# Seven-product FFN input on one Trainium2 core: Silu as one ScalarE function, a bank sum done by TensorE, no arithmetic on POOL, casts issued ahead of functions

## The chip, the cores and the metric

The kernel runs on one core of a Trainium2 chip. Its engines are called as in the profile: PE (matmul) with its weight loads PEld, DVE (VectorE), ACT (ScalarE), POOL (GpSimd) and SP, which only issues transfers. The metric is the device time of one execution in microseconds (us); of several runs the median counts.

## The reference, cut to what matters

One decoder layer over 512 tokens and 1024 channels, in float32: a hybrid mixer, then a SwiGLU FFN with 2816 hidden channels. The change is in the FFN's first half, in the end of the mixer that feeds it, and in one line for a row of the FFN's second half.

```
x = x + gate1 * rms_norm(mix_out, g_post_mix)
h2 = rms_norm(x, g_pre_ffn) * (1 + scale2) + shift2
gt, up = split(h2 @ w_ffn_in, 2)          # 1024 -> 2 x 2816
f = (silu(gt) * up) @ w_ffn_out
x = x + gate2 * rms_norm(f, g_post_ffn)
```

## The kernel before, in words

Every float32 product is made of three float32r matmuls (`mm3`, L156): each operand is taken apart into a rounded high part, cast by ACT, and the rest, a subtraction on DVE (`split`, L152 to 154: the cast is L153, the subtraction L154). So each piece of weights costs a cast of 128x1024 and a subtraction of 128x1024 before PE can use it. High and low parts live in tiles `whi` and `wlo`, four buffers each.

**The stage of the change.** `h2 @ w_ffn_in` is done in 11 units `u` of 2 x 128 hidden channels (gate and up columns together). A unit is a 2x2 by 2x2 block product (two halves of the 1024 inputs, two halves of the tokens, two column blocks), and it is done in seven block products instead of eight. A product is one call `step(u, q, ...)`, q = 1 to 7: 24 matmuls of 128x256 at L1185 into one bank of PSUM. The order of the 77 products is written out by hand in `WINO` (L243). Counted from 0, steps 0 to 13 belong to units 0 and 1 and the first two products of unit 2, step 14 is (u=0, q=3), and from step 27 on seven steps per unit run in one fixed order.

- The weights of a unit come by DMA from SP's queue (`wino_load`, L257) into four blocks. Products 1, 2, 4 use a block as it is. Products 5, 6 and 3 use a running sum `wsum` of blocks: first the sum of two (L281), then two more, each added by an accumulating DMA that POOL issues (L302). Product 7 uses a block to which another was added (`wsum3`, L285).
- `step` first prepares a later piece (`split_to`, cast and subtraction), then runs `flush()` for what was put off, then its 24 matmuls.
- The token side: `hbh`/`hbl` hold four blocks of token parts; `tx` holds the parts of three combinations that are built from `ta` (the tile `tar`) and `b22` (tile `b`) while the first products run.
- The results: `gated` (L1189) makes silu(g)*u as Exp, Ln(1+.), Exp on ACT (`sigm`, L163 to 165: g's sigmoid), then two DVE products put off to the next step (L1194, L1195). `gated_m1` (L1206) combines three banks on DVE (c, L1209 to 1212) ahead of it. In the loop over units from 3 on, product 1 is copied to the SBUF tile `u` by ACT (L1367), and product 6 is taken from it by DVE (L1374).

**Ahead of the stage** the last two of four token blocks leave the mixer's output projection: `chain_sq`, `chain_norm`, `chain_x1` (L1091 the residual, L1095 its product with the scale row, named `xm`), `chain_norm2`, `chain_h2` (L1104) and four transposes per half (`h2_tr`). For block 2 both `xm` products run on POOL, for block 3 one of them. In the first units the sums L281 and L285 and the combinations L1312 and L1327 run on POOL too; from unit 2 on L281 and L285 run on DVE.

**Behind the stage** the FFN's second half, `f @ w_ffn_out`, runs over two halves of the output columns. During the first one a generator `mods_in_turn` (L972) makes the row of gate2 in two pieces; a `pump()` after each pair of weight blocks (24 matmuls of 128x512) lets it go on to its next `yield`. It adds up `macc` on DVE (L1002), has a bias added by an accumulating DMA from POOL (L1008), splits the result (`mah`) and multiplies it with ones on PE (L979, tile `pmr`). At the very end, for each of four token blocks, ACT makes Square sums, Ln (L1442) and Exp (L1444), DVE two products (L1447), and the result goes out.

The order on PE, DVE, ACT and POOL is that of the program in this stage (`manual_schedule`); each engine runs its instructions in that order. Where an instruction waits, all behind it on its engine waits as well.

## Time and profile before

| what | value |
|---|---|
| median of 3 runs | 853.81 us (849.71 to 855.4) |
| the profiled execution | 852.54 us, span 850.8 us |
| mean granted PE clock | 0.972 |
| PE busy | 771.2 us, 91% |
| DVE busy | 570.2 us, 67% |
| ACT busy | 423.1 us, 50% |
| POOL busy | 165.7 us, 19% |

The span is the time from the first to the last instruction; the execution lies 1.7 us around it. Busy time of PE counts overlapping, pipelined matmuls, so a busy PE isn't a PE at its peak; the number of matmuls that a stretch holds tells more. PEclk is the share of its clock that PE was granted. In rows of instructions the order is start and duration (us), engine, line, operation, output <- input, and in brackets how long the engine had been idle and who released it. In rows that group instructions the order is line, engine, operation, names and shapes, count, then busy us and mean ns of one, then idle time before them and who ended it.

### The profile page before, as it was taken

How to read it: one execution, taken by the hardware profiler on the slowest of the kernel's cores; microseconds unless marked ns; L12 is line 12 of the kernel's file. 1: busy time of each engine (PE TensorE's matmuls, PEld its weight loads, DVE VectorE, ACT ScalarE, POOL GpSimd, SP SyncE). 2: the span in 40 equal slices, each digit the busy share in tenths (PEclk: the TensorE clock that was granted, in tenths of full speed). 3: DMA queues.
4: the chain of work that ended last, by engine and by line, in shares of the span. 5: the costliest groups of instructions: out<-in, count | busy, mean ns of one | idle time of the engine just before them, and what ended most of it. 6: DMA issues, size and time to landing. Idle time of an engine off the chain costs nothing. (4 is left out here: it accounts for less than half of the span.)

```text
span 850.8 us, 11361 instructions
## 1 busy us (share of the span) xinstructions
PE 771.2 (91%) x4357; PEld 659.6 (78%) x4357; DVE 570.2 (67%) x808; ACT 423.1 (50%) x710; POOL 165.7 (19%) x200
## 2 busy tenths in 40 slices
PE   3899999999999999999975759999898889879996
PEld 3679887776788888888875659989888888768885
DVE  5989867568566664557878766767766767673214
ACT  5466544666674554516743534644455456333112
POOL 4353423244311111030035201111110110000000
PEclk9999999999999999999988869999999999999999
DMA  9962332214146877567652464666555444652202
GB/s 281 302 213 75 123 99 59 86 55 148 50 131 228 217 242 210 178 155 260 201 133 49 75 149 99 149 149 148 134 122 123 95 99 161 219 184 80 75 1 99
DMA packets 119462, 120.37 MB, mean 141 GB/s; under 512 B 4012, under 2 KB 93152, under 8 KB 119408
## 3 DMA queue, kind: packets, MB, share of 16 engines
q1 hardware_dynamic: 109072, 99.63, 38.2%
q0 software_dynamic: 9568, 18.96, 12.0%
q10 hardware_dynamic: 768, 1.07, 0.3%
q8 instruction: 34, 0.56, 0.3%
q14 instruction: 20, 0.16, 0.1%
HBM read 102.33 MB, written 2.10 MB: 123 GB/s over the span
## 5 line engine op out<-in xcount | busy, mean ns | idle before, releaser
L154 DVE TENSOR_TENSOR wlo<-wraw,whi 128x1024 fp32r<-128x1024 f32 (+1 forms) x129 | 160.6, 1251 | 125.0 <-ACT whi L153 124.9
L153 ACT CAST whi<-wraw 128x1024 fp32r<-128x1024 f32 (+1 forms) x129 | 132.3, 1031 | 132.7 <-PE pgt L158 33.2
L1185 PE MATMUL pf<-hbh,whi 128*128 128x256 f32 x352 | 101.9, 290 | 19.4 <-ACT hbh L153 9.7
L1185 PE MATMUL pf<-tx,whi 128*128 128x256 f32 x528 | 99.7, 290 | 12.7 <-ACT whi L153 9.0
L1185 PE MATMUL pf<-hbh,wlo 128*128 128x256 f32 x352 | 100.7, 286 | 4.5 <-DVE wlo L154 4.5
L1185 PE MATMUL pf<-hbl,whi 128*128 128x256 f32 x352 | 100.4, 285 | 1.8 <-DVE hbl L154 1.7
L1185 PEld LDWEIGHTS pf<-tx,whi 128*128 128x128 f32 x528 | 84.4, 196 | 13.6 <-ACT whi L153 9.4
L1185 PEld LDWEIGHTS pf<-hbh,whi 128*128 128x128 f32 x352 | 68.0, 193 | 22.5 <-ACT hbh L153 9.9
L1185 PE MATMUL pf<-tx,wlo 128*128 128x256 f32 x264 | 77.8, 295 | 7.0 <-DVE wlo L154 7.0
L157 PE MATMUL pgt<-hh,whi 128*128 128x512 f32 x192 | 75.8, 395 | 0.0
L159 PE MATMUL pgt<-hh,wlo 128*128 128x512 f32 x192 | 75.4, 393 | 0.0
L158 PE MATMUL pgt<-hl,whi 128*128 128x512 f32 x192 | 74.8, 389 | 0.0
L1185 PEld LDWEIGHTS pf<-hbh,wlo 128*128 128x128 f32 x352 | 67.8, 193 | 5.8 <-DVE wlo L154 5.8
L1185 PEld LDWEIGHTS pf<-hbl,whi 128*128 128x128 f32 x352 | 68.0, 193 | 2.4 <-DVE hbl L154 2.3
L302 POOL DMA_DIRECT2D wsum<-wraw x22 | 26.4, 1200 | 220.2 <-DVE wlo L154 211.0
L157 PE MATMUL pfo<-whi,fparts 128*128 128x512 f32 x154 | 61.2, 398 | 0.0
L158 PE MATMUL pfo<-wlo,fparts 128*128 128x512 f32 x154 | 61.2, 398 | 0.0
L159 PE MATMUL pfo<-whi,fparts 128*128 128x512 f32 x154 | 61.0, 396 | 0.0
L1185 PEld LDWEIGHTS pf<-tx,wlo 128*128 128x128 f32 x264 | 51.5, 195 | 10.5 <-DVE wlo L154 10.5
L154 DVE TENSOR_TENSOR wlo<-wsum,whi 128x1024 fp32r<-128x1024 f32 x33 | 40.2, 1222 | 17.0 <-ACT whi L153 17.0
L1002 DVE SCALAR_TENSOR_TENSOR macc<-wraw,sc,macc 128x512 f32<-128x512 f32 x56 | 42.8, 765 | 10.0 <-ACT macc L1000 5.5
L153 ACT CAST whi<-wsum 128x1024 fp32r<-128x1024 f32 x33 | 33.7, 1045 | 29.6 <-DVE wsum L281 21.1
(400 smaller groups left out, 1723.3 us busy)
## 6 DMA issues: line engine op xcount, KB each, us to landing
wraw<-in_w_in_dram SPq DMA_DIRECT2D x20, 1024.0 KB, 5.2
wraw<-in_w_ffn_in_dram SPq DMA_DIRECT2D x40, 512.0 KB, 5.9
wraw<-in_mod_w_dram SPq DMA_DIRECT2D x16, 1024.0 KB, 5.9
wsum<-wraw POOLq DMA_DIRECT2D x22, 512.0 KB, 5.9
...
wraw<-in_mod_w_dram SPq DMA_DIRECT2D x16, 512.0 KB, 6.5
...
gate<-gate POOLq DMA_DIRECT2D x14, 256.0 KB, 4.2
```

What stands on the lines that cost most here:

```text
L153: act.copy(hi, src)
L154: vec.tensor_tensor(lo, src, hi.bitcast(F32), ALU.subtract)
L157: pe.matmul(o, whi, xhi, start=start, stop=False)
L158: pe.matmul(o, whi, xlo, start=False, stop=False)
L159: pe.matmul(o, wlo, xhi, start=False, stop=stop)
L302: nc.gpsimd.dma_start(un["s"], un[0][q - 5], accum_op=ALU.add)
L1002: vec.scalar_tensor_tensor(acc, mw[:, r], c_, acc, op0=ALU.mult, op1=ALU.add)
L1185: pe.matmul(o[:, cs], a_[:, g, k, :], b_, start=(start and g + k + part == 0), stop=(stop and k == 3 and part == 2), skip_group_check=True)
```

## The change

It has seven parts.

1. **Silu.** `gated` calls one ACT function, Silu, and one DVE product; before it was three functions and two products. The function itself is put off to the next `flush`, its product to the one after. A table of functions with Silu is loaded once in the stage.
2. **The bank sum.** From unit 3 on ACT copies bank p1 to a fresh bank p6, product 6 accumulates onto it, and ACT copies the sum to SBUF. The DVE subtraction is gone; the sign goes into the token combination `ta`. Products 2 and 7 trade places.
3. **No arithmetic on POOL.** The `xm` products and the combinations of `ta` go to DVE. For units 0 and 1 the sums L281 and L285 become DMAs: SP loads one block straight into the `wsum` tile, POOL issues accumulating DMAs for the rest.
4. **Casts ahead of functions.** `split(..., True)` issues only the cast and puts the subtraction off to the next `lows()`; `begin(n)` prepares the pieces up to number n at the place where it stands. So in the first units casts stand on ACT ahead of functions and copies that came before them.
5. **Order.** The first six products are taken as (0,1), (1,1), (0,2), (2,1), (1,2), (2,2), and some of units 2 and 3 trade places. The sums of unit 2 and later are made one piece ahead.
6. The generator for the gate2 row waits one more `yield` between the DMA of its bias and its split.
7. With another table of functions loaded in between, the build places table loads before each Ln and each Exp at the end of the kernel.

Where the lines of the changed kernel differ from those before, L1225 is the Silu, L1226 its product, L155 the cast, L157 and L159 the subtraction, L1427 and L1434 the copies of the bank, L301, L302 and L315 the accumulating DMAs, L1488 the Square sums, L1503 and L1505 Ln and Exp.

POOL's queue over the whole stage, before:

```order
L1095 TENSOR_TENSOR xm<-x_3361,SHSC 128x512 x3
L281 TENSOR_TENSOR wsum<-wraw 128x1024
L302 DMA wsum<-wraw 128x2x512
L281 TENSOR_TENSOR wsum<-rawf 128x1024
L302 DMA wsum<-wraw 128x2x512
L285 TENSOR_TENSOR wraw<-wraw 128x2x512
L1312 TENSOR_TENSOR tar<-tar,b_3803 128x512 x2
L285 TENSOR_TENSOR rawf<-rawf,wraw 128x1024
L302 DMA wsum<-wraw 128x2x512
L1327 TENSOR_TENSOR tar<-braw,tar 128x512 x2
L302 DMA wsum<-wraw 128x2x512 x19
```

and of the change:

```order
L301 DMA wsum<-wraw 128x2x512
L302 DMA wraw<-wraw 128x2x512
L301 DMA wsum<-rawf 128x1024
L302 DMA rawf<-wraw 128x2x512
L315 DMA wsum<-wraw 128x2x512 x22
```

The eleven operations on tiles are gone, and 26 accumulating DMAs stand where 22 stood.

ACT in the loop over units, around unit 6 (three functions each for one block of 512 and two of 256 columns, with the casts of pieces between), before:

```order
L163 ACTIVATE sg_5722<-c_5718 128x512
L164 ACTIVATE sg_5722<-sg_5722,one_c 128x512
L165 ACTIVATE sg_5722<-sg_5722 128x512
L153 CAST whi<-wraw 128x1024
L163 ACTIVATE sg_5756<-pf_5588 128x256
L164 ACTIVATE sg_5756<-sg_5756,one_c 128x256
L165 ACTIVATE sg_5756<-sg_5756 128x256
L153 CAST whi<-wraw 128x1024
L153 CAST whi<-wsum 128x1024
L163 ACTIVATE sg_5823<-u_5589 128x256
L164 ACTIVATE sg_5823<-sg_5823,one_c 128x256
L165 ACTIVATE sg_5823<-sg_5823 128x256
```

and of the change, one whole unit (end of unit 4 to unit 5):

```order
L1225 ACTIVATE sg_4974<-pf_4839 128x256
L155 CAST whi<-wraw 128x1024
L1225 ACTIVATE sg_5011<-c_5000 128x512
L155 CAST whi<-wsum 128x1024
L155 CAST whi<-wraw 128x1024
L1225 ACTIVATE sg_5074<-u_4939 128x256
L1427 COPY pf_5100<-pf_5069 128x512
L155 CAST whi<-wraw 128x1024
L155 CAST whi<-wsum 128x1024
L1434 COPY u_5169<-pf_5100 128x512
L155 CAST whi<-wsum 128x1024
L155 CAST whi<-wraw 128x1024
```

Nine functions became three, one copy became two, and no three functions in a row stand between two casts any more.

ACT at the end of the kernel, for the last token block, before:

```order
L1427 ACTIVATE tt,so<-pfo3a 128x256
L1427 ACTIVATE tt,so<-pfo3b 128x256
L1442 ACTIVATE so<-so 128x1
L1444 ACTIVATE so<-so 128x1
L1452 DMA out_dram<-x_3361 128x512
```

and of the change:

```order
L1488 ACTIVATE tt,so<-pfo3a 128x256
L1488 ACTIVATE tt,so<-pfo3b 128x256
L1503 ACT_TABLE_LOAD
L1503 ACTIVATE so<-so 128x1
L1505 ACT_TABLE_LOAD
L1505 ACTIVATE so<-so 128x1
L1513 DMA out_dram<-x_3361 128x512
```

Two table loads per token block are new, eight in all.

The diff, cut to its core:

```diff
-    def split(hi, lo, src):
+    lows_ = []
+
+    def split(hi, lo, src, defer=False):
         act.copy(hi, src)
-        vec.tensor_tensor(lo, src, hi.bitcast(F32), ALU.subtract)
+        if defer:
+            lows_.append(lambda: vec.tensor_tensor(lo, src, hi.bitcast(F32), ALU.subtract))
+        else:
+            vec.tensor_tensor(lo, src, hi.bitcast(F32), ALU.subtract)
+
+    def lows():
+
+        while lows_:
+            lows_.pop(0)()
...
-    WINO = [(u, q) for u in range(3) for q in (1, 2)]
+    WINO = [(0, 1), (1, 1), (0, 2), (2, 1), (1, 2), (2, 2)]
     WINO += [(u, q) for q in (5, 7, 6, 4) for u in range(2)]
-    WINO += [(0, 3), (2, 5), (1, 3), (2, 4), (2, 7), (2, 6)]
-    WINO += [(3, 5), (3, 1), (3, 4), (2, 3), (3, 6), (3, 7), (3, 2)]
+    WINO += [(0, 3), (2, 5), (1, 3), (2, 4), (3, 5), (2, 6), (3, 1), (2, 7), (3, 4), (2, 3)]
+    WINO += [(3, q) for q in (6, 2, 7)]
     for u in range(4, NU):
-        WINO += [(u, 5), (u - 1, 3)] + [(u, q) for q in (1, 4, 6, 7, 2)]
+        WINO += [(u, 5), (u - 1, 3)] + [(u, q) for q in (1, 4, 6, 2, 7)]
...
+    def wsum_tile():
+        return late_pool["fx"].tile([P, 2, 512], F32, tag="wsum", name="wsum", bufs=2)
+
+    def wsum(u):
+
         un = units[u]
-        un["s"] = late_pool["fx"].tile([P, 2, 512], F32, tag="wsum", name="wsum", bufs=2)
-        eng.tensor_tensor(un["s"], un[1][0], un[1][1], ALU.add)
-
-    def wsum3(u, eng):
+        un["s"] = wsum_tile()
+        if u > 1:
+            vec.tensor_tensor(un["s"], un[1][0], un[1][1], ALU.add)
+            return
+        for g in range(2):
+            nc.sync.dma_start(un["s"][:, g].rearrange("p (k n) -> p k n", k=4),
+                              wino_src(u, 1, g)[:, 0:4])
+        nc.gpsimd.dma_start(un["s"], un[1][1], accum_op=ALU.add)
+        nc.gpsimd.dma_start(un[1][0], un[0][0], accum_op=ALU.add)
+
+    def wino_piece(u, q, defer=False):
         un = units[u]
-        eng.tensor_tensor(un[1][0], un[1][0], un[0][0], ALU.add)
-
-    def wino_piece(u, q):
-        un = units[u]
-        for i in range(2 if u > 2 else q in (1, 2)):
+        for i in (1, 0) if u > 2 and q != 3 else range(q in (1, 2)):
             if i not in un:
                 wino_load(u, i)
-        if q == 5 and u > 1:
-            wsum(u, vec)
-        if u > 1 and q == (7 if u == 2 else 4):
-            wsum3(u, vec)
         src = {1: (0, 0), 2: (0, 1), 4: (1, 1), 7: (1, 0)}.get(q)
         src = un[src[0]][src[1]] if src else un["s"]
         hi = wp.tile([P, 1024], FR, tag="whi", name="whi").rearrange("p (g n) -> p g n", g=2)
         lo = wp.tile([P, 1024], FR, tag="wlo", name="wlo").rearrange("p (g n) -> p g n", g=2)
-        split(hi, lo, src)
+        split(hi, lo, src, True)
         if q in (5, 6):
-            nc.gpsimd.dma_start(un["s"], un[0][q - 5], accum_op=ALU.add)
+            lows_.append(lambda: nc.gpsimd.dma_start(un["s"], un[0][q - 5], accum_op=ALU.add))
+        if not defer:
+            lows()
+
+        i = WINO.index((u, q)) + 1
+        nxt = WINO[i] if i < len(WINO) else (0, 0)
+        if nxt[1] == 5 and nxt[0] > 1:
+            for k in (1, 0) if nxt[0] > 2 else ():
+                if k not in units[nxt[0]]:
+                    wino_load(nxt[0], k)
+            wsum(nxt[0])
+        if u > 1 and q == 6:
+            vec.tensor_tensor(un[1][0], un[1][0], un[0][0], ALU.add)
...
             nc.gpsimd.dma_start(acc[0:1, :], mod_b[n0:n0 + 512].unsqueeze(0), accum_op=ALU.add)
             yield
+            if not rest:
+                yield
             am = parts_()
             split(*am, acc)
...
-    def chain_x1(tb, pos, junk, engs=(vec, vec)):
-        st, xms[tb] = sts[tb], []
-        xvs = [x1[:, tb, half(hf)] for hf in range(2)]
-        for hf, xv in enumerate(xvs):
+    def chain_x1(tb, pos, junk):
+        st = sts[tb]
+        for hf in range(2):
+            xv = x1[:, tb, half(hf)]
             vec.scalar_tensor_tensor(xv, pos[hf], st[:, 2:3], xv, op0=ALU.mult, op1=ALU.add)
             act.activation(junk(), xv, AF.Square, accum_out=st[:, 3 + hf:4 + hf])
-        for hf, xv in enumerate(xvs):
-            xms[tb].append(q2("xm"))
-            engs[hf].tensor_tensor(xms[tb][hf], xv, SC[hf], ALU.mult)
+
+    def chain_xm(tb):
+        xms[tb] = [q2("xm") for _ in range(2)]
+        for hf in range(2):
+            vec.tensor_tensor(xms[tb][hf], x1[:, tb, half(hf)], SC[hf], ALU.mult)
...
+        go, later[:] = later[:], []
+        for f_ in go:
+            f_()
...
-        sigm(sg, g)
-
-        def products():
-            vec.tensor_tensor(dst, sg, g, ALU.mult)
-            vec.tensor_tensor(dst, dst, u, ALU.mult)
-        later.append(products)
+        def function():
+            s_ = sg()
+            act.activation(s_, g, AF.Silu)
+            later.append(lambda: vec.tensor_tensor(dst, s_, u, ALU.mult))
+        later.append(function)
...
+        def begin(n):
+
+            while at["split"] < wino0 + n:
+                split_piece(True)
...
+        act.preload_act_table_set("silu_and_others")
+        fresh(5)
         tx_tiles(7)
         for u in range(2):
             vec.tensor_tensor(k4(t3_, u), k4(b22, u), pts[u][0], ALU.subtract)
-            parts_of(7, t3_, u)
-        for u in range(2):
-            pool.tensor_tensor(k4(ta, u), k4(ta, u), k4(b22, u), ALU.add)
-        f4s.append(f4_tile("f4"))
-        gated_m0(f4s[0], pb_[1][0], 0)
-        fresh(5, 3)
-        wsum3(1, pool)
-        for u in range(1, 3):
+            parts_of(7, t3_, u, True)
+        lows()
+        begin(9)
+        for u in range(3):
             f4s.append(f4_tile("f4"))
             gated_m0(f4s[u], pb_[1][u], 0)
             flush()
-        fresh(5, 3)
...
+            vec.scalar_tensor_tensor(k4(ta, u), k4(ta, u), -1.0, k4(b22, u), op0=ALU.mult,
+                                     op1=ALU.subtract)
...
+            vec.tensor_tensor(k4(ta, u), raws2[1, u], k4(ta, u), ALU.add)
...
+            p6 = bank("pf6")
+            act.copy(p6, p1)
             p4 = bank("pf4")
             step(u, 4, p4, True, True)
             if u == 3:
-                third()
-            p6 = bank("pf6")
-            step(u, 6, p6, True, True)
-            vec.tensor_tensor(u2, u2, p6, ALU.subtract)
+                third_of(2, pb_[5][2], u2s[2])
+            step(u, 6, p6, False, True)
+            u2 = temp("u2", 512, 2)
+            act.copy(u2, p6)
+            step(u, 2, p1, False, True)
+            gated_m0(f4s[u], p1, 0)
             p7 = bank("pf7")
             step(u, 7, p7, True, True)
             gated_m1(f4s[u], p4, p5, p7, u2)
-            step(u, 2, p1, False, True)
-            gated_m0(f4s[u], p1, 0)
-            third = lambda args=(u, p5, u2): third_at(*args)
+            third = lambda a_=(u, p5, u2): third_of(*a_)
```

139 lines of the change are left out of this document (80 added, 59 removed).

## The prediction

> **What bounds the kernel now.** I read the share of each engine first (PE busy 91% of the span), then cut the span into stages and read the busy time of every engine in each.
>
> ```profile
> core 0: us, PE busy (x) PEld busy (x) DVE busy (x) ACT busy (x) POOL busy (x), PEclk, DMA share, GB/s
> 425.87:510.84 84.97, 54.83 (x375) 52.48 (x373) 60.19 (x68) 36.65 (x68) 24.96 (x16) 0.80 0.45 100
> 519.34:547.60 28.26, 28.26 (x242) 28.26 (x241) 21.48 (x27) 13.71 (x19) 3.60 (x3) 1.00 0.76 159
> 547.60:711.30 163.70, 148.31 (x1182) 141.50 (x1181) 115.28 (x140) 84.54 (x123) 15.61 (x13) 1.00 0.56 131
> 570.90:594.20 23.30, 21.14 (x170) 20.15 (x169) 16.48 (x20) 11.69 (x18) 2.40 (x2) 1.00 0.60 136
> 711.30:850.80 139.50, 126.51 (x600) 103.50 (x598) 64.30 (x81) 42.98 (x70) 2.79 (x4) 0.98 0.32 110
> ```
>
> The second row holds steps 18 to 27 of the FFN input, ten times 24 matmuls, without a gap: 28.26/10 = 2.826 us is what a step costs when PE never waits. All 77 steps and two times eight transposes (1.04 us each, below) would take 220 us. They take 285 (425.87 to 711.30), so 65 us of this stage aren't PE's own work, in two parts. Steps 0 to 14, the first row, take 85 us instead of 44. Steps 28 to 76, the third, take 163.7 instead of 49 x 2.826 = 138.5, though DVE (115 of 163.7) and ACT (85) are far from full: there PE waits for the latency of a chain, not for an engine's rate. What it waits for, in the first part and then in the second:
>
> ```profile
> PE pf L1185 <- ACT hbh L153: 9.7, 1, 9.7
> PE pf L1185 <- ACT whi L153: 8.8, 1, 8.8
> PE pf L1185 <- ACT u L1268: 5.2, 2, 4.5
> ...
> PE pf L1185 <- DVE wlo L154: 10.7, 20, 0.9
> PE pf L1185 <- ACT whi L153: 3.7, 7, 0.6
> ```
>
> In the first part the waits have a price beyond themselves: after one, PE runs at half its clock.
>
> ```profile
> 469.29 0.80 PE L1185 MATMUL pf<-tx,whi 128*128 128x256 f32 x2 [8.81 <-ACT whi L153]
> 506.16 0.58 PE L1185 MATMUL pf<-hbh,whi 128*128 128x256 f32 x1 [9.65 <-ACT hbh L153]
> 505.00:510.00 5.00, 3.70 (x15) 3.41 (x16) 3.21 (x4) 2.05 (x3) 0.00 (x0) 0.50 0.01 3
> ```
>
> Step 14 goes on at 506.16 and step 15 starts at 510.84, the end of the first row: 4.7 us for most of a step. What made the 8.8 us is seen on DVE and POOL:
>
> ```profile
> 457.46 8.22 DVE L154 TENSOR_TENSOR tx<-t3r,tx 128x256 fp32r<-128x256 f32 x2 [0.47 <-ACT tx L153]
> 466.75 0.43 DVE L154 TENSOR_TENSOR tx<-t3r,tx 128x256 fp32r<-128x256 f32 x1 [0.47 <-ACT tx L153]
> L1312 POOL TENSOR_TENSOR tar<-tar,b 128x512 f32<-128x512 f32 x2 | 2.9, 1701 | 0.0
> L285 POOL TENSOR_TENSOR wraw<-wraw 128x1024 f32<-128x1024 f32 x1 | 2.9, 2857 | 0.0
> L285 POOL TENSOR_TENSOR rawf<-rawf,wraw 128x1024 f32<-128x1024 f32 x1 | 2.8, 2762 | 0.0
> ```
>
> Two subtractions that take 0.43 us each take 8.22 us while POOL runs those three groups (8.6 us) without a break. DVE stands still behind POOL, ACT waits for DVE, PE for both.
>
> **The change part by part: steps 0 to 14.** Without POOL's arithmetic DVE has more to do and no stall. Its durations in this stretch, and three rows that the count needs:
>
> ```profile
> 410.11 1.04 PE L1112 MATMUL pt<-ident,xm 128*128 128x128 f32 x8
> ...
> 424.52 1.22 DVE L154 TENSOR_TENSOR wlo<-wraw,whi 128x1024 fp32r<-128x1024 f32 x1
> ...
> 428.12 0.20 ACT L1077 ACTIVATION_READ_ACCUMULATOR sq<-pwo 128x1 f32 x1
> ...
> L154 DVE TENSOR_TENSOR wlo<-wsum,whi 128x1024 fp32r<-128x1024 f32 x8 | 9.7, 1223 | 4.3 <-ACT whi L153 4.3
> L154 DVE TENSOR_TENSOR tx<-tar,tx 128x256 fp32r<-128x256 f32 x8 | 2.9, 419 | 0.0
> L1104 DVE SCALAR_TENSOR_TENSOR xm<-xm,st,SHSC 128x512 f32<-128x512 f32 x4 | 2.8, 747 | 2.4 <-ACT st L150 2.4
> L1212 DVE TENSOR_TENSOR c<-pf,c 128x512 f32<-128x512 f32 x2 | 1.4, 692 | 0.2
> L1194 DVE TENSOR_TENSOR f<-sg,pf 128x256 f32<-128x256 f32 x3 | 1.3, 419 | 2.1 <-ACT sg L165 2.1
> ```
>
> Step 14 needs the second half of `hbl` from `b22`, which stands on DVE behind both chains c of units 0 and 1. From 425.7, where the subtraction for step 1 ends (424.52 + 1.22), I count what stands on DVE up to there: 14 subtractions of 128x1024 (14 x 1.22 = 17.1); one sum `wsum` (1.2); of 128x512 four xm, two products with G, eight token combinations (`tar`, `t3r`), four hbl, two u, six c, one f, 27 in all (27 x 0.69 = 18.6); seven with a scalar operand, four h2 and three x1 (7 x 0.75 = 5.2); twelve subtractions for tx (12 x 0.42 = 5.0); three f of 256 (1.3); three tiny ones (0.5). The sum is 48.9 us, so step 14 can't go on before 474.6. PE's own steps end earlier (13 x 2.826 + 2 x 1.04 from 428.7, the end of step 0, is 467.5): DVE is the bound here.
>
> The other end: DVE was idle for 84.97 - 60.19 = 24.8 us of this stretch; if all of that stays, step 14 goes on at 499.4. I walked the written order and put 6 us of waits on DVE, near the early end: 0.5 for the cast of product (0,2), 1.1 for the cast after `wsum` of unit 2, 1 for the table load of Silu, 3 for the second bank of sums. That last one is new: SP may load the `wsum` tiles once DVE's first product with G for block 3 has run, about 429.3 now (the squares ahead of it end at 428.3); twelve issues follow, and then POOL's accumulating DMAs, the third of which makes the sum for product (1,5).
>
> ```profile
> rawf<-in_w_ffn_in_dram SPq DMA_DIRECT2D x8, 256.0 KB, 5.0
> wsum<-wraw POOLq DMA_DIRECT2D x2, 512.0 KB, 5.1
> ```
>
> Its inputs are issued by 434.5 and land by 439.5, and 1.2 us of queue and 5.1 more make 446, where ACT asks for it at 444.5. So step 14 goes on at 480.5 instead of 506.16: **-25.7 us** (-31.6 to -6.8). The wait before it is still some 8 us and costs the half clock once more, in the same size as before. Steps 6 and 8 keep small gaps.
>
> **Steps 15 to 76.** The functions and DVE operations of one unit, before:
>
> ```profile
> L153 ACT CAST whi<-wraw 128x1024 fp32r<-128x1024 f32 x4 | 4.1, 1036 | 0.0
> L164 ACT ACTIVATE sg<-sg,one_c 128x512 f32<-128x512 f32 x2 | 1.4, 724 | 0.1
> L163 ACT ACTIVATE sg<-c 128x512 f32<-128x512 f32 x1 | 0.6, 632 | 4.1 <-DVE c L1212 4.1
> L163 ACT ACTIVATE sg<-u 128x256 f32<-128x256 f32 x1 | 0.4, 420 | 4.3 <-DVE u L1217 4.3
> L1367 ACT COPY u<-pf 128x512 f32<-128x512 f32 x1 | 0.6, 578 | 0.0
> ```
>
> Silu has no row here; an Exp of the same shape has, and Ln is the dearest, so one Silu costs 0.4 (256) and 0.63 to 0.72 (512). ACT loses two functions of three blocks (about 2.8 us), gains a copy (0.6): 11.7 to 9.5 us per unit. DVE loses three products (0.42 + 0.42 + 0.69) and the subtraction of the bank (0.69): 16.5 to 14.3. What counts is the order. With a step at 2.826, a unit at 19.8, counted from the start of its first step: product c from 0.2 to 2.3, Silu to 3.1, cast for product 6 to 4.2 and its subtraction to 5.4, the block sum to 6.6, f and u to 8.0; the copy to p6 ends at 9.3 and PE wants it at 11.3; the copy out of p6 ends at 15.0, the cast for product 3 at 16.1, its subtraction at 17.3, wanted at 22.6; the next unit's casts are ready 4 to 6 us ahead. Every piece comes early, so nothing but PE sets the pace. Steps 15 to 76 then take 62 x 2.826 = 175.2 us instead of 711.30 - 510.84 = 200.5: at most 25.3. I take **-24**, one less for the last unit, in which two f parts of 128x1024 are cast in between. If half of the waits stayed, it would be -12.
>
> The transfers stay what they were, 3.17 MB per unit (23.3 us at 136 GB/s in the row of one unit), now in 19.8 us: 160 GB/s, as in the second row of the first fence.
>
> **The second half of the FFN.** PE waits twice for the gate2 row:
>
> ```profile
> PE pmr L979 <- ACT mah L153: 6.3, 2, 4.4
> PE pmr L980 <- DVE mah L154: 0.2, 1, 0.2
> ```
>
> One more pump between the bias DMA and the split is 24 matmuls of 128x512, 5.6 us, more than the longest wait. The seven yields fit into the eight pumps. **-5.5** (-6.5 to 0, if the transfer of the gate weights is late instead).
>
> **The end.** A table load has one row, the one at the start; the end of the last block is:
>
> ```profile
> 0.81 1.28 ACT L60 ACT_TABLE_LOAD   x1 [0.81 <-PEq L1466]
> 844.88 0.20 ACT L1427 ACTIVATION_READ_ACCUMULATOR tt<-pfo3b 128x1 f32 x1
> 845.52 0.29 ACT L1442 ACTIVATE so<-so 128x1 f32<-128x1 f32 x1 [0.44 <-DVE so L1436]
> 845.85 0.20 ACT L1444 ACTIVATE so<-so 128x1 f32<-128x1 f32 x1
> ```
>
> The first load may start at 845.1 and ends at 846.4, Ln at 846.7, the second load at 848.0, where Exp started at 845.85: **+2.1** (0 to +2.6). The loads of the three blocks before fit between their matmuls. The Trainium skill, "ScalarE: Activation LUTs", section "What ACT_TABLE_LOAD costs", speaks against the change here: each switch of the set costs the load, the 1.28 us of the row above, and another 1.38 us of draining. By it Exp would start at 850.7, the end would cost +4.9 instead of +2.1, and the time would be 2.8 us more. The row can't tell, since what follows it waits for a DMA. I keep the row.
>
> **Sum.** -25.7 - 24 - 5.5 + 2.1 = -53.1. The profiled execution took 852.54, so 799.4; the median of the runs is 1.3 above it: **801 us**.
>
> **The rivals.** (A) The transfers replace POOL: the sums of units 0 and 1 now wait for a load and for two accumulating DMAs in a row instead of 2.4 to 2.9 us of POOL. For it: 3 MB of loads and 2 MB of sums meet in some 16 us. Against it: two of these sums landed in 5.1 us. If each landed twice as late, DVE would stand 5 to 10 us more ahead of step 7, and with the late end above it is up to 19: 806 to 820, say 812. The Trainium skill's "SBUF — State Buffer", section "SBUF: two separate sides", names a way to it: POOL writes the descriptors of its own DMAs, and can't while DVE, in one of its two-port modes, holds the port that they share. By it such a sum would land late beside DVE's work in such a mode; the 5.1 us don't show it.
>
> (B) The loop stays half latency-bound, because ACT's copies of banks wait for PE in the middle of the queue, with casts behind them. For it: ACT is in order, and two copies per unit now wait for the end of a step. Against it: pieces have 4 to 6 us to spare. 801 + 12 = 813.
>
> (C) Slower: transfers become the bound of the loop. A unit needs 3.17 MB; all else that is gained is 29 us, 4.2 per unit over seven units, so from 23.3 + 4.2 = 27.5 us per unit on, that is below 115 GB/s, the kernel is slower than before. At 100 GB/s, the rate over steps 0 to 14, a unit takes 31.7: 852.5 - 29 + 7 x 8.4 + 1.3 = 884. Against it: 159 GB/s in the second row, with PE never waiting.
>
> (D) No change: what PE waits for is only named differently, and the chain through POOL's queue and DVE is as long as before. Then the time stays within 1%. The 8.22 us row speaks against it.
>
> **How the numbers follow.** Forecast 0.60, A 0.20, B 0.11, C 0.04, D 0.05. Three runs of the kernel before spread over 5.7 us, 0.7%; about 1% is what a measurement can tell from no change. Forecast, A and B are all faster by more: 0.91; same 0.05; slower 0.04. The forecast with its early ends is 801 - 5.9 - 1.3 - 1 = 793; A and B reach 820 each. The range is 792 to 821.
>
> **What would show it.** Right: no TENSOR_TENSOR on POOL from 425 us on, tx subtractions at 0.4 us throughout, step 14 going on near 480 with one cold stretch, some 19.8 us from unit to unit with no wait of PE on wlo, no wait on mah, the last Exp 2 us later. Wrong: PE waiting on casts of `wsum` that a DMA releases (A), waits on whi or wlo in the loop (B), a DMA share near 1 there (C), DVE still idle for 20 us ahead of step 14.

## The result and the profile after

| | before | after |
|---|---|---|
| median of the runs | 852.15 us (849.71 to 855.4) | 807.99 us (805.7 to 811.08) |
| ratio after to before | | 0.9482 (95%: 0.9431 to 0.9533) |
| profiled execution | 852.54 us, span 850.8 | 806.69 us, span 804.5 |

The kernel became faster by 5.2% (4.7 to 5.7), 45.9 us between the two profiled executions where 53.1 were forecast. I cut the span of the changed kernel at the same places as that of before: steps 0 to 14, steps 15 to 76, the second half of the FFN up to its last matmul, and what follows it.

```profile
core 0: us, PE busy (x) PEld busy (x) DVE busy (x) ACT busy (x) POOL busy (x), PEclk, DMA share, GB/s
424.43:485.32 60.89, 49.54 (x377) 47.91 (x375) 47.80 (x70) 32.30 (x59) 10.44 (x9) 0.92 0.92 199
485.32:664.31 178.99, 176.78 (x1491) 175.99 (x1490) 130.95 (x145) 85.21 (x108) 20.06 (x17) 1.00 0.64 151
664.31:788.04 123.73, 123.73 (x600) 102.70 (x598) 54.33 (x65) 40.99 (x55) 2.80 (x4) 1.00 0.30 103
788.04:804.50 16.46, 0.27 (x3) 0.07 (x1) 5.03 (x11) 7.66 (x14) 0.00 (x0) 0.63 0.26 96
```

The last two stretches of before, cut in the same way, are

```profile
711.30:844.05 132.75, 126.24 (x599) 103.42 (x598) 61.91 (x75) 41.64 (x64) 2.79 (x4) 0.99 0.32 107
844.05:850.80 6.75, 0.28 (x3) 0.08 (x1) 2.39 (x6) 1.34 (x6) 0.00 (x0) 0.80 0.41 153
```

The first number behind the window is its length. Against the forecast's terms this gives:

| stretch | forecast | measured |
|---|---|---|
| steps 0 to 14 (84.97 before) | -25.7 | -24.1 |
| steps 15 to 76 (200.46 before) | -24 | -21.5 |
| second half, first to last matmul (132.75 before) | -5.5 | -9.0 |
| last matmul to the end (6.75 before) | +2.1 | **+9.7** |
| the stage starts 1.44 earlier; 0.45 more around the span | | -1.0 |
| sum | -53.1 | -45.9 |

The first three terms together are right within a microsecond (-54.6 measured, -55.2 forecast), but only as a sum: two fell short by 1.6 and 2.5 us, and the third gave 3.5 more than forecast. What is missing of the gain is at the end of the program. These are PE's waits in the first two stretches, to be read against those of before (9.7, 8.8, 5.2 and so on in the first, 10.7 and 3.7 in the second):

```profile
PE pf L1217 <- ACT hbh L155: 4.7, 2, 4.1
PE pf L1217 <- DVE hbl L159: 2.7, 1, 2.7
PE pf L1217 <- DVE wlo L157: 1.9, 3, 1.0
PE pf L1217 <- ACT whi L155: 1.0, 1, 1.0
PE pf L1217 <- DVE hbl L157: 1.0, 1, 1.0
...
PE pf L1217 <- DVE c L1241: 1.6, 1, 1.6
PE pf L1217 <- ACT pf L1427: 0.6, 2, 0.4
```

The wait of 8.8 us ahead of product 7 is gone, and POOL has no arithmetic in this stretch. The one ahead of step 14 is left, now in two pieces, and so is its cold stretch: step 14 goes on at 480.71, the matmul there takes 0.58 us, and step 15 starts 4.6 us later.

```profile
477.65 0.39 PE L1217 MATMUL pf<-hbh,whi 128*128 128x256 f32 x1 [4.10 <-ACT hbh L155]
480.71 0.58 PE L1217 MATMUL pf<-hbl,whi 128*128 128x256 f32 x1 [2.67 <-DVE hbl L159]
```

In the second stretch 1.6 us of wait stand at the last step of the last unit, and two short ones at the copied bank. In the second half of the FFN PE waits for nothing any more: its busy time is the whole window, 123.73 of 123.73.

**The end** is read on ACT. The first of the four token blocks of before, up to the first square of the second block, and the same rows of the changed kernel:

```profile
831.88 0.60 ACT L1427 ACTIVATE tt<-pfo 128x512 f32<-128x512 f32 x1 [8.70 <-PE pfo L159]
833.45 0.29 ACT L1442 ACTIVATE so<-so 128x1 f32<-128x1 f32 x1 [0.88 <-DVE so L1436]
833.77 0.20 ACT L1444 ACTIVATE so<-so 128x1 f32<-128x1 f32 x1
835.45 0.37 ACTq L1452 DMA_DIRECT2D out_dram<-x  x1
836.08 0.60 ACT L1427 ACTIVATE tt<-pfo 128x512 f32<-128x512 f32 x1 [2.10 <-PE pfo L159]
```

```profile
775.86 0.60 ACT L1488 ACTIVATE tt<-pfo 128x512 f32<-128x512 f32 x1 [8.70 <-PE pfo L169]
777.41 1.28 ACT L1503 ACT_TABLE_LOAD   x1 [0.86 <-DVE so L1497]
778.71 0.30 ACT L1503 ACTIVATE so<-so 128x1 f32<-128x1 f32 x1
779.02 1.28 ACT L1505 ACT_TABLE_LOAD   x1
780.32 0.20 ACT L1505 ACTIVATE so<-so 128x1 f32<-128x1 f32 x1
782.00 0.38 ACTq L1513 DMA_DIRECT2D out_dram<-x  x1
782.42 0.60 ACT L1488 ACTIVATE tt<-pfo 128x512 f32<-128x512 f32 x1 [1.90 <-DVE x L1508]
```

Before, the next block's square is released by PE, 4.20 us after the first (836.08 - 831.88). Now it is released by DVE's x of the block before, 6.56 us after the first. The four blocks form one chain on ACT: the issue of the output's transfer stands on ACT's queue, it waits for x, and the next square stands behind it. Without loads that chain is 3.94 us per block (from 831.88 to the end of the issue, 835.45 + 0.37), so it had 0.26 us to spare, though the row shows a wait of 2.10 for PE. Two loads make it 3.94 + 2 x 1.28 = 6.50. The first squares of the four blocks start at 831.88, 836.08, 840.28 and 844.24 us before, and at 775.86, 782.42, 788.97 and 795.48 now. So the first three blocks pass on 2.36, 2.35 and 2.55 us, and the last block's own two loads make the rest of the 9.7, 2.45.

### The profile page after: what moved, and what is told of

It reads as the page before. It is cut to its first block, busy times and chain, and to the rows that moved or that the text cites. A ratio compares the mean times of both kernels' runs of the same rounds, so it can differ in the third digit from the quotient of the medians.

```text
span 804.5 us, 11296 instructions
## 1 busy us (share of the span) xinstructions
PE 753.6 (94%) x4357; PEld 650.4 (81%) x4357; DVE 540.9 (67%) x774; ACT 407.3 (51%) x661; POOL 149.4 (19%) x193
## 4 chain that ended last, share of the span: by engine, by line
PE 74%; DVE 10%; DMA 7%; ACT 5%; issue 2%; POOL 2%; SPq 0%; ACTq 0%; DVEq 0%; POOLq 0%
PE pf L1217 19%; PE pgt L167 5%; PE pgt L169 5%; PE pgt L168 5%; PE pfo L169 4%; PE pfo L168 4%; PE pfo L167 4%; DMA wsum<-wraw 2%; PE pwo L168 2%; PE pwo L169 2%; PE pwo L167 2%; PE pbr L167 2%; PE pbr L169 2%; PE pbr L168 2%; DVE smacc L356 2%
## 5 line engine op out<-in xcount | busy, mean ns | idle before, releaser
L155 ACT CAST whi<-wraw 128x1024 fp32r<-128x1024 f32 (+1 forms) x129 | 133.0, 1034 | 161.4 <-PE pgt L168 35.0
L159 DVE TENSOR_TENSOR wlo<-wraw,whi 128x1024 fp32r<-128x1024 f32 (+1 forms) x89 | 109.9, 1242 | 85.1 <-ACT whi L155 84.7
L1217 PE MATMUL pf<-tx,whi 128*128 128x256 f32 x528 | 95.3, 282 | 0.6 <-ACT pf L1427 0.6
L1217 PEld LDWEIGHTS pf<-tx,whi 128*128 128x128 f32 x528 | 80.9, 188 | 1.2 <-ACT pf L1427 1.2
L1217 PE MATMUL pf<-tx,wlo 128*128 128x256 f32 x264 | 74.4, 282 | 1.2 <-DVE wlo L157 1.2
L157 DVE TENSOR_TENSOR wlo<-wsum,whi 128x1024 fp32r<-128x1024 f32 x33 | 40.4, 1225 | 35.5 <-ACT whi L155 35.1
L155 ACT CAST whi<-wsum 128x1024 fp32r<-128x1024 f32 x33 | 34.5, 1049 | 54.8 <-DVE wsum L296 19.4
L315 POOL DMA_DIRECT2D wsum<-wraw x22 | 26.0, 1180 | 180.4 <-DVE wlo L157 180.4
L157 DVE TENSOR_TENSOR wlo<-wraw,whi 128x1024 fp32r<-128x1024 f32 x40 | 48.8, 1220 | 10.2 <-ACT whi L155 10.2
L1217 PEld LDWEIGHTS pf<-tx,wlo 128*128 128x128 f32 x264 | 49.7, 188 | 1.6 <-DVE wlo L157 1.6
```

The costliest lines, as they stand in the source:

```text
L155: act.copy(hi, src)
L157: lows_.append(lambda: vec.tensor_tensor(lo, src, hi.bitcast(F32), ALU.subtract))
L159: vec.tensor_tensor(lo, src, hi.bitcast(F32), ALU.subtract)
L315: lows_.append(lambda: nc.gpsimd.dma_start(un["s"], un[0][q - 5], accum_op=ALU.add))
L1217: pe.matmul(o[:, cs], a_[:, g, k, :], b_, start=(start and g + k + part == 0), stop=(stop and k == 3 and part == 2), skip_group_check=True)
```

## The experiments

All runs are compared by the same four pieces, each the difference of two rows of PE's timeline or of a row and the span: (a) from the first matmul of step 0 to the matmul at which step 14 goes on, (b) from there to the first matmul of the second half, (c) from there to the last matmul, (d) from there to the end of the span.

| kernel | median us | ratio to before (95%) | a | b | c | d |
|---|---|---|---|---|---|---|
| before | 852.15 | | 80.29 | 205.14 | 132.75 | 6.75 |
| after | 807.99 | 0.948 (0.943-0.953) | 56.28 | 183.60 | 123.73 | 16.46 |
| e1_one_load | 799.11 | 0.939 (0.935-0.942) | 55.46 | 183.26 | 123.74 | 6.74 |
| e2_three_functions | 809.20 | 0.951 (0.948-0.953) | 61.34 | 189.39 | 123.73 | 6.72 |
| e3_one_pump | 805.40 | 0.948 (0.944-0.952) | 55.74 | 182.37 | 123.88 | 16.53 |
| e4_pool_sums | 808.89 | 0.950 (0.947-0.952) | 57.56 | 182.51 | 123.74 | 16.25 |
| e6_no_bank_sum | 807.32 | 0.946 (0.943-0.949) | 55.57 | 182.47 | 123.72 | 16.52 |
| e7_before_no_pool | 844.49 | 0.989 (0.986-0.992) | 72.18 | 205.81 | 132.96 | 6.44 |
| e10_functions_first | 812.17 | 0.952 (0.949-0.955) | 58.63 | 185.59 | 123.73 | 16.46 |
| e11_before_silu | 818.32 | 0.959 (0.956-0.962) | 73.32 | 181.64 | 129.55 | 6.75 |
| e8_b22_first | 789.78 | 0.927 (0.925-0.929) | 52.73 | 181.87 | 123.74 | 6.74 |
| e9_all | 788.57 | 0.925 (0.923-0.927) | 50.91 | 180.87 | 123.73 | 6.77 |
| e12_casts_at_steps | 808.76 | 0.948 (0.946-0.951) | 57.04 | 182.81 | 123.72 | 16.54 |
| e13_before_silu_no_pool | 811.84 | 0.952 (0.950-0.955) | 66.32 | 180.88 | 129.28 | 6.46 |

### The end: one load instead of eight

```diff
         f_split(1)
         third()
         flush()
+        act.preload_act_table_set("natural_log_exp_and_others")
     flush()
```

> The changed kernel, with the function set of Ln and Exp loaded once on ACT, behind the last Silu. Theory 1: in the changed kernel the eight table loads stand in a serial chain of four blocks, each block's first square on ACT behind the block before; without them the blocks' squares are 4.20 us apart as in the kernel before (6.56 now) and from the last matmul's start to the end of the span it is 6.8 us instead of 16.5. Time 808.0 - 9.7 = 798 (797 to 800). Theory 2, the prediction's own sum: the loads of the first three blocks lie between their matmuls and only the last block's two count. Time 808.0 - 2.1 = 806.

799.11 us, 8.9 below the changed kernel, and piece (d) is 6.74, what it was before the change. Theory 1 holds: the whole loss at the end was the eight loads. ACT's waits in the tail, of this kernel:

```profile
ACT tt L1489 <- PE pfo L169: 12.9, 3, 8.7
ACT so L1504 <- DVE so L1498: 3.1, 4, 0.9
ACT tt L1489 <- DVE x L1509: 1.9, 1, 1.9
```

Three of the four first squares wait for PE again, and one for DVE's x. The load that was put in, 1.28 us at 664.90, lies ahead of a wait of 5.59 us of ACT for a transfer.

### The loop: the single function, the order, the bank sum

```diff
         def function():
             s_ = sg()
-            act.activation(s_, g, AF.Silu)
-            later.append(lambda: vec.tensor_tensor(dst, s_, u, ALU.mult))
+            sigm(s_, g)
+
+            def products():
+                vec.tensor_tensor(dst, s_, g, ALU.mult)
+                vec.tensor_tensor(dst, dst, u, ALU.mult)
+            later.append(products)
...
-        act.preload_act_table_set("silu_and_others")
```

> The changed kernel with the sigmoid made of Exp, Ln and Exp and two products on DVE, as before the change, and so no load of another set. Theory 1: the loop (steps 15 to 76) gained by the order of the work, and ACT and DVE have room in it: those steps still take 179 us (within 2), the end is 9.7 us shorter, steps 0 to 14 are 1 to 3 us longer, since DVE has three more products of 128x256 there. Time 808.0 - 9.7 + 2 = 800 (798 to 803). Theory 2: the single function made the loop's gain of 21.5 us; then a good part of it goes, 10 us or more, and the time is 808 to 820.

809.20 us: (d) is 9.7 shorter, as expected, but (a) is 5.1 and (b) 5.8 longer. Neither theory had it whole. With three functions the rest of the change, its order above all, brings 15.8 of the 21.5 us that piece (b) gained. PE's waits from step 15 on, of this kernel:

```profile
PE pf L1217 <- ACT pf L1430: 4.0, 7, 1.2
PE pf L1217 <- DVE c L1245: 2.0, 2, 1.6
```

Now the copied bank is what PE waits for, in seven of the eight units of the loop: ACT's copy stands behind the functions. Whether the order would bring more without that copy, no run shows.

The other half of this question is the kernel before with the single function alone, and one load on each side of it:

```diff
     def gated(dst, g, u, sg):
-        sigm(sg, g)
-
-        def products():
-            vec.tensor_tensor(dst, sg, g, ALU.mult)
-            vec.tensor_tensor(dst, dst, u, ALU.mult)
-        later.append(products)
+        act.activation(sg, g, AF.Silu)
+        later.append(lambda: vec.tensor_tensor(dst, sg, u, ALU.mult))
...
+        act.preload_act_table_set("silu_and_others")
         tx_tiles(7)
...
         f_split(1)
         third()
+        act.preload_act_table_set("natural_log_exp_and_others")
```

> The kernel before with one thing changed: Silu as a single function of ACT and one product on DVE, its set loaded once ahead of the first and the set of Ln and Exp loaded once behind the last (two loads, no end of its own to pay). Theory 1: what the single function gives does not hang on the order: 5 us in steps 0 to 14, 5.6 in the loop, and the waits for the gate row of the FFN's second half go with it, 9.0: 852 - 20 = 832 (828 to 836). Theory 2: the loop before is bound by the latency of its chain, in which two functions of three are 0.9 to 1.4 us for each of three blocks; it gains 2 to 3 us for each of eight units, and with the rest the time is 852 - 5 - 20 - 9 = 818 (814 to 824). Theory 3: the order is what counts, and the function alone gives under 10 us: 842 or more.

818.32 us, theory 2. The function alone gives 33.8 us, and piece (b) falls by 23.5, which is 2.0 more than in the changed kernel: with the single function in place, the rest of the change costs this stretch a little (the copied bank, see e6_no_bank_sum below, and a wait of 1.6 us at the last step, which isn't there in e11_before_silu). The loop in the old order, with the functions ahead of the casts and DVE's subtraction in it, from 503 us to its end:

```profile
503.00:680.40 177.40, 177.40 (x1498) 177.40 (x1496) 133.01 (x151) 78.47 (x100) 20.39 (x17) 0.99 0.65 146
```

PE is busy for the whole window. So the loop was held up by the length of the function chain on ACT, with the next casts behind it. This row of before, for the loop from 547.6 to 700 us, fits. DVE's subtractions wait for ACT's casts 19 times, and ACT's functions in turn for DVE's u and c (30.2 and 24.8 us): a chain that goes to and fro between two engines, neither of them full.

```profile
DVE wlo L154 <- ACT whi L153: 43.2, 19, 3.1
```

Silu also takes one DVE product away from each block (0.42 or 0.69 us, beside 0.93 to 1.36 us of functions), and no run separates the two. Either cure alone brings most of the gain (15.8 by the order, 23.5 by the function), and they don't add up, since PE's own work is the floor under both.

```diff
-        def function():
-            s_ = sg()
-            act.activation(s_, g, AF.Silu)
-            later.append(lambda: vec.tensor_tensor(dst, s_, u, ALU.mult))
-        later.append(function)
+        s_ = sg()
+        act.activation(s_, g, AF.Silu)
+        later.append(lambda: vec.tensor_tensor(dst, s_, u, ALU.mult))
```

> The changed kernel with each Silu issued at once where its argument is made, and not behind the casts of the next step. Theory 1: the order of casts ahead of functions makes what the loop gained beyond the single function: three functions in the same order cost 5.6 us of its 21.5, so some 16 are the order's; with the functions first ACT waits for DVE's c with the casts behind it, and the loop takes 10 us or more longer, 818 to 824. Theory 2: with one short function the order matters little, since a wait of ACT for c is 1 to 3 us and the casts have 4 to 6 us to spare: 808 to 811.

812.17 us, 4.2 more than the changed kernel, 2.4 of it in (a) and 2.0 in (b): near theory 2. With the single function in place, the order of casts and functions is worth some 4 us, half of it in the loop. The intervals of the two ratios overlap (0.949 to 0.955, and 0.943 to 0.953), so this rests on the pieces of one profiled execution each.

```diff
-            p6 = bank("pf6")
-            act.copy(p6, p1)
+            p6, u2 = bank("pf6"), temp("u2", 512, 2)
+            act.copy(u2, p1)
...
-            step(u, 6, p6, False, True)
-            u2 = temp("u2", 512, 2)
-            act.copy(u2, p6)
+            step(u, 6, p6, True, True)
+            vec.tensor_tensor(u2, p6, u2, ALU.add)
```

> The changed kernel without the bank sum in the loop of units 3 to 10: ACT copies the bank of product 1 out, product 6 starts a bank of its own and DVE adds the two. Theory 1: nothing in the loop waits for DVE long enough, PE's pace stays, and the two short waits for the copied bank (0.38 and 0.22 us) go; steps 15 to 76 take 177 to 180 us as now (179) and the time stays at 808 within 2. Theory 2: the copied bank is what took DVE's operation off a chain that PE waits for; without it 1 to 2 us per unit come back, 816 to 824.

807.32 us and (b) 1.1 shorter than in the changed kernel: theory 1. The bank sum on TensorE takes 0.69 us per unit off an engine that nobody waits for (DVE is busy for 131 of 179 us), and gives nothing.

### Steps 0 to 14: POOL's arithmetic, the sums by transfer, the casts

In the kernel before, only this (each of the eight places in steps 0 to 14 and just ahead of them):

```diff
-        chain_x1(2, pos[2], lambda: t2("sq2"), (pool, pool))
+        chain_x1(2, pos[2], lambda: t2("sq2"))
...
-        wsum(0, pool)
+        wsum(0, vec)
...
-        wsum3(0, pool)
+        wsum3(0, vec)
...
-            pool.tensor_tensor(k4(ta, u), k4(ta, u), k4(b22, u), ALU.add)
+            vec.tensor_tensor(k4(ta, u), k4(ta, u), k4(b22, u), ALU.add)
```

> The kernel before, and in it only the arithmetic of POOL in steps 0 to 14 and ahead of them given to DVE (three products with the norm's row, four sums of weights, four token combinations). DVE gains 9.8 us of work and loses 13.5 us of standing still, by the rows of before that are longer than others of their shape (8.22, 4.47, 3.25, 0.97 and 1.83 us). Theory 1, the prediction's: the still time is what PE waits for; the waits of 8.8 us ahead of product 7 and part of 9.7 ahead of step 14 go, steps 0 to 14 are 8 to 14 us shorter, time 838 to 844. Theory 2, after the run with POOL's sums, which cost nothing against the transfers: DVE's work takes the place of its standing still, and what is left is 13.5 - 9.8 = 3.7 us: 848 (846 to 852).

844.49 us, 8.0 less, all of it in (a) (8.1): half a microsecond above theory 1's range, and far from theory 2. The wait ahead of product 7 went from 8.81 to 2.67 us, the one ahead of step 14 only from 9.65 to 8.73.

The reverse in the changed kernel: POOL's arithmetic in place of the accumulating transfers.

```diff
-        for g in range(2):
-            nc.sync.dma_start(un["s"][:, g].rearrange("p (k n) -> p k n", k=4),
-                              wino_src(u, 1, g)[:, 0:4])
-        nc.gpsimd.dma_start(un["s"], un[1][1], accum_op=ALU.add)
-        nc.gpsimd.dma_start(un[1][0], un[0][0], accum_op=ALU.add)
+        nc.gpsimd.tensor_tensor(un["s"], un[1][0], un[1][1], ALU.add)
+        nc.gpsimd.tensor_tensor(un[1][0], un[1][0], un[0][0], ALU.add)
```

> The changed kernel with the sums of units 0 and 1 (four of 128x1024) made by POOL's arithmetic again and not by accumulating transfers. Theory 1: DVE stands still while POOL adds; four sums of some 2.4 to 2.9 us cost DVE 11 us, from which 6.5 us of its waits behind the transfers' sums come off. Step 15 starts 4.5 us later: 808.0 + 4.5 = 812.5 (810 to 816), and single DVE rows of 2 to 8 us show in the stretch. Theory 2: the late transfers' sums (waits of 2.85 and 3.84 us on ACT, of 2.48 and 4.06 us on DVE) cost more than POOL did; then step 15 starts up to 4 us earlier, 804.

808.89 us: no difference, (a) 1.3 longer. Neither theory's size came, and the rows show why. POOL and DVE of this kernel:

```profile
432.37 2.40 POOL L298 TENSOR_TENSOR wsum<-wraw 128x1024 f32<-128x1024 f32 x1 [48.16 <-PE pf L1214]
434.86 2.68 POOL L299 TENSOR_TENSOR wraw<-wraw 128x1024 f32<-128x1024 f32 x1
437.49 2.80 POOL L298 TENSOR_TENSOR wsum<-rawf 128x1024 f32<-128x1024 f32 x1
440.38 3.24 POOL L299 TENSOR_TENSOR rawf<-rawf,wraw 128x1024 f32<-128x1024 f32 x1
```

```profile
433.16 4.93 DVE L1130 SCALAR_TENSOR_TENSOR xm<-xm,st,SHSC 128x512 f32<-128x512 f32 x2
438.01 3.37 DVE L157 TENSOR_TENSOR wlo<-wraw,whi 128x1024 fp32r<-128x1024 f32 x1
441.30 2.33 DVE L1125 TENSOR_TENSOR st<-st 128x1 f32<-128x1 f32 x1
```

DVE does stand still while POOL adds: rows that take 1.41, 1.22 and 0.15 us in the changed kernel take 7.9 us more. But they come early, where DVE had time (from 425 to 450 us it is busy for 23.92 us here and for 17.11 in the changed kernel), and ACT waits for none of these four sums. In the changed kernel ACT waits for the transfers instead:

```profile
442.10 1.05 ACT L155 CAST whi<-wsum 128x1024 fp32r<-128x1024 f32 x1 [2.85 <-DMA wsum<-wraw]
447.99 1.04 ACT L155 CAST whi<-wsum 128x1024 fp32r<-128x1024 f32 x1 [3.84 <-DMA wsum<-rawf]
```

The transfers that make these sums, of the changed kernel from 425 to 450 us (number, KB each, median us to landing), are the reason:

```profile
wsum<-wraw POOLq DMA_DIRECT2D x2, 512.0 KB, 9.3
wraw<-wraw POOLq DMA_DIRECT2D x1, 512.0 KB, 11.5
wsum<-rawf POOLq DMA_DIRECT2D x1, 512.0 KB, 9.7
rawf<-wraw POOLq DMA_DIRECT2D x1, 512.0 KB, 12.3
```

They take 9.3 to 12.3 us, where the prediction's row of before had 5.1. That row held two of the five accumulating transfers in steps 0 to 14 of before; the five took 5.0 to 8.3 us, with a median of 5.9. One late sum was exchanged for another.

The casts of these steps, issued at the steps again and not at written places:

```diff
-            while at["split"] < wino0 + n:
+            while n < 3 and at["split"] < wino0 + n:
                 split_piece(True)
...
-        def fresh(q, ahead=0):
+        def fresh(q, ahead=3):
...
-        step(0, 2, pb_[1][0], False, True, 0)
+        step(0, 2, pb_[1][0], False, True, 3)
```

(and so for `sixth` and the second and third of these steps)

> The changed kernel with the casts of steps 0 to 14 issued as before the change: not at written places (from the third on), but at each step for the third step ahead. Of the 24 us that steps 0 to 14 gained, the single function alone gave 7.0 and POOL's arithmetic alone 8.1 in the kernel before; 9 are left. Theory 1: they are the written order of the casts; without it those steps take 70 us instead of 61: 817 (813 to 820). Theory 2: they are the changed order of the chains and of the token combinations, and the casts cost 0 to 3: 808 to 811.

808.76 us, (a) 0.8 longer: theory 2. The written places of the casts are worth nothing that can be measured.

Both parts that did count, together in the kernel before (the edits of e11_before_silu and e7_before_no_pool):

> The kernel before with both of e11 and e7: the single function with one load behind it, and POOL's arithmetic given to DVE; every order as before. Theory 1: the two act on different waits and add up: 852 - 34 - 8 = 810 (807 to 813), and steps 0 to 14 take 85 - 7 - 8 = 70 us. Theory 2: both shorten the one chain ahead of product 7 and step 14, and what one gives the other can't: 814 to 818.

811.84 us, theory 1: (a) falls by 14.0, against 7.0 and 8.1 alone. In piece (a) 10.0 us of the changed kernel's gain of 24.0 are left (66.32 to 56.28). They aren't the casts (e12_casts_at_steps) and aren't the sums by transfer (e4_pool_sums). The largest difference that meets the eye is at step 1. Before, and in e13_before_silu_no_pool too, step 1 is product (0,2), which goes on in the bank of product (0,1), so it must wait until ACT has copied that bank; and the copy stands behind a norm that waits for DVE. These are ACT's rows of before:

```profile
432.36 0.29 ACT L149 ACTIVATE st<-st,eps_c 128x1 f32<-128x1 f32 x1 [2.69 <-DVE st L1082]
432.68 0.20 ACT L150 ACTIVATE st<-st 128x1 f32<-128x1 f32 x1
432.79 0.57 ACT L1268 COPY u<-pf 128x512 f32<-128x512 f32 x1
```

Step 2 starts 13.6 us after step 0 there (439.43 - 425.87), and 13.5 in e13_before_silu_no_pool. In the changed kernel step 1 is product (1,1) with a bank of its own, and step 2 starts after 5.7 us (430.08 - 424.43), 7.9 us earlier.

But this lead isn't what is left at step 14. In e4_pool_sums, which has the new order as well, PE loses nearly all of it again beside POOL's additions: step 4 starts 19.0 us after step 0, against 20.2 in e13_before_silu_no_pool and 12.1 in the changed kernel. Its step 14 still goes on 8.8 us earlier than in e13_before_silu_no_pool (57.56 against 66.32) and only 1.3 later than in the changed kernel. The lead of the changed kernel itself is down to 4.7 us at step 8 and grows to 11.1 at step 13. Of this growth 2.8 us are PE's wait at step 12, 3.0 us in e13_before_silu_no_pool and 0.2 in the changed kernel:

```profile
476.67 0.38 PE L1185 MATMUL pf<-tx,whi 128*128 128x256 f32 x1 [1.45 <-ACT tx L153]
478.62 0.39 PE L1185 MATMUL pf<-tx,whi 128*128 128x256 f32 x1 [1.56 <-DVE tx L154]
474.66 1.05 ACT L153 CAST whi<-wsum 128x1024 fp32r<-128x1024 f32 x1 [4.16 <-DMA wsum<-wraw]
```

In e13_before_silu_no_pool ACT waits there for a late sum, with the casts of the token parts for step 12 behind it; in the changed kernel these casts come first. So the 10 us belong to the new order of steps 0 to 14 as a whole. Which part of it gives how much, no run shows.

### The second half: the pump

```diff
             yield
-            if not rest:
-                yield
             am = parts_()
```

> The changed kernel without the second pump between the bias transfer and the split of the gate row. Theory 1: PE waits twice for mah again, 6.5 us in all, and runs at half clock after the longer wait, as the stretch from the first to the last matmul of the FFN's second half shows, 132.75 us before and 123.73 after. Time 808.0 + 9.0 = 817 (815 to 818). Theory 2: the waits alone count, 808.0 + 6.5 = 814.5. Theory 3: the transfers of the gate weights come earlier for other reasons, and the pump does nothing: 808.

805.40 us, theory 3: the second pump does nothing here, (c) is 123.88, and PE never waits for `mah`. The chain of the gate row simply starts earlier. The first row below is ACT's first operation on the gate row in the kernel before, the second the same in e3_one_pump:

```profile
720.75 0.72 ACT L1000 ACTIVATE macc<-wraw,sc 128x512 f32<-128x512 f32 x1
```

```profile
665.78 0.72 ACT L1025 ACTIVATE macc<-wraw,sc 128x512 f32<-128x512 f32 x1
```

Counted from the first matmul of the second half it comes at 9.45 us before (711.30) and at 2.39 in e3_one_pump (663.39). The functions of the last unit stand ahead of it on ACT, and the whole chain of the gate row is 7 us earlier. Both the order and the function have a part in that: the same operation comes at 3.77 us in e2_three_functions (new order, long functions, 681.02 - 677.25) and at 6.50 in e11_before_silu (old order, single function, 686.90 - 680.40). In e11_before_silu, with neither the pump nor the new order, one wait of 3.56 us is left (and 0.2 behind it), so the function alone isn't enough. In e2_three_functions PE doesn't wait, but the pump is in there; whether the order alone would be enough, no run shows.

### Two versions beyond the change

Step 14 waits for the split of `b22`, which needs nothing that comes late and merely stands behind the chain c on DVE and ACT. On top of e1_one_load:

```diff
         sixth(3)
+        for u in range(2):
+            act.copy(hbh[:, 2, :, tks[u]], k4(b22, u))
+        split_to(wino0 + 15)
+        for u in range(2):
+            vec.tensor_tensor(hbl[:, 2, :, tks[u]], k4(b22, u),
+                              hbh[:, 2, :, tks[u]].bitcast(F32), ALU.subtract)
         for u in range(2):
             fresh(4, 4 - u)
...
-            split(hbh[:, 2, :, tks[u]], hbl[:, 2, :, tks[u]], k4(b22, u))
```

> The changed kernel with the one load of e1, and the split of b22's second operand moved: both casts on ACT ahead of the cast for product (0,3), both subtractions on DVE behind the sum for unit 2 and ahead of the chains c of units 0 and 1. Theory 1, that step 14 waits for its place in DVE's queue: it goes on when DVE has read the bank of product (0,5), 475.7 in the times of the changed kernel instead of 480.7, the cold stretch is shorter, and the time is that of e1, 799.1, less 5 to 6: 794 (792 to 796). Theory 2, that DVE's rate is the bound: the steps behind wait for their own casts instead, and 797 to 800 stays.

```profile
477.75 0.36 PE L1217 MATMUL pf<-hbh,whi 128*128 128x256 f32 x1 [2.25 <-DVE c L1241]
```

789.78 us, 0.927 of before (0.925 to 0.929) against 0.939 (0.935 to 0.942) of e1_one_load. PE's wait ahead of step 14 is 2.25 us instead of 6.7, it is for DVE's reading of a bank now, as expected (though step 14 goes on at 477.75 and not at 475.7), and the matmul behind it takes 0.36 us instead of 0.58: steps 0 to 14 take 55.5 us instead of 60.1 (425.02 to 480.53; 424.70 to 484.77 in e1_one_load). These 4.6 us are what the profile accounts for. The profiled executions are 3.8 apart (796.03 and 792.21), but the medians 9.3, and 789.78 is below theory 1's range of 792 to 796; what the rest of the gain is, the traces don't show.

Last, on top of that, the sums of unit 1 by DVE:

```diff
-        if u > 1:
+        if u > 0:
             vec.tensor_tensor(un["s"], un[1][0], un[1][1], ALU.add)
+            if u == 1:
+                vec.tensor_tensor(un[1][0], un[1][0], un[0][0], ALU.add)
             return
...
-            if u < 2:
+            if u < 1:
                 wsum(u)
...
         t1_of(1)
+        wsum(1)
         step(2, 2, pb_[1][2], False, True, 0)
```

> As e8, and the two sums of unit 1 made by DVE ahead of the cast for product (1,5) instead of by a load and two accumulating transfers. Theory 1: ACT's wait of 3.84 us for that sum and DVE's 4.06 behind it go, against 2.3 us of DVE's work, and all behind it comes 2 us earlier: 792 (789 to 795), below e8. Theory 2, after the run with POOL's sums: what makes the sum does not matter, the same as e8 within 1.

788.57 us, ratio 0.925 (0.923 to 0.927). Piece (a) is 1.8 shorter than in e8_b22_first, as theory 1 has it, but the two intervals overlap, so by time it isn't told from theory 2. This is the fastest version: 19 us below the changed kernel, with three small edits.

## Why the prediction was right, and where it was not

**The total.** 801 was forecast and 808 measured, inside the range of 792 to 821, and the sign and most of the size came out. The step that failed is the sentence "The loads of the three blocks before fit between their matmuls". I took the wait of 2.10 us on ACT's row for spare time. It was not: 1.85 us of it passed while ACT's queue held the issue of an output transfer, which isn't counted as busy, and 0.26 us were free. The term is +9.7 and not +2.1, shown by e1_one_load; these 7.6 us are what the forecast lacked, and the other errors nearly cancel. The Trainium skill, "ScalarE: Activation LUTs", section "What ACT_TABLE_LOAD costs", would add 1.38 us of draining to each load of 1.28. The rows don't agree: the function starts 0.02 us behind its load (777.41 + 1.28, and 778.71), and a block with two loads takes 6.52 us to the end of its issue (782.00 + 0.38 - 775.86), 2.58 more than 3.94, which is 2 x 1.28 and 0.02.

**Steps 0 to 14.** The time came out within 0.2 us (step 14 goes on at 480.71, forecast 480.5) by luck: two errors cancel. I counted 48.9 us of DVE's work up to there and put 6 us of waits on it. DVE is busy for 43.1 us in that window, and idle for 11.8:

```profile
425.70:480.65 54.95, 43.66 (x344) 42.02 (x342) 43.12 (x66) 31.46 (x58) 10.44 (x9) 0.95 0.98 210
451.40 1.42 DVE L157 TENSOR_TENSOR tx<-t3r,tx 128x256 fp32r<-128x256 f32 x4
```

The work was too much since neighbouring rows overlap (four subtractions for tx take 1.42 us together, not 4 x 0.42). The waits were too few mainly since the sums by transfer took 9.3 to 9.7 us and not 5.1, which was the time of the two quickest of five before: DVE's two waits behind these sums are 2.48 and 4.06 us, where I had put 3. That is the mechanism of rival A at the low end of its price (5.8 us more idle time, where A had 5 to 10), hidden by the first error. e4_pool_sums shows that the transfers gained next to nothing over POOL's additions in the same places (1.3 us in (a)). That POOL holds DVE up was right (rows of e4_pool_sums, 8.1 us in e7_before_no_pool). The Trainium skill's "SBUF — State Buffer", section "SBUF: two separate sides", has a reason for it, a pair of ports that DVE and GpSimd share and that one instruction holds to its end; the stretched rows of 4.93 and 3.37 us, each beside POOL's additions, agree. But POOL was a third of the gain. The single function was 7 us of it, and some 10 us belong to the new order of these steps, which had no term of its own in my prediction and which no run takes apart.

**Steps 15 to 76.** The time is right: 178.99 us, PE never waiting but for 2.2 us; some 1 us of the missing 2.5 is the copied bank with its slow matmuls behind (1.1 by e6_no_bank_sum), the rest the last unit and a step of 2.835 instead of 2.826 us. The reason was half right. "What counts is the order": with three functions the order does bring 15.8 us. But it isn't needed: e11_before_silu has the old order and loses nothing, and e10_functions_first, with the new function and the old order of casts and functions, loses 2 us. What held the loop up was the length of the function chain, which the prediction had, as ACT's gain of 2.8 us per unit, and passed over for the order. In an order that puts the next casts behind the functions, that chain was the latency.

**The second half.** -9.0 instead of -5.5: the waits were 6.5 us, and most of the rest is the slow matmuls behind them (after the wait of 4.4 us they follow each other at 0.43 us, and elsewhere at 0.23), which I left out. And the pump, which the term was hung on, isn't needed: e3_one_pump.

**Rivals.** B and C did not come: no wait on whi or wlo in the loop, and a DMA share of 0.64 there. A came in part.
